# Dilated attention in a hybrid decoder layer: a head's combination in twelve pieces, regroup copies one per two groups, a pool for w_out's raw tiles, and ones-products of one convolution tile moved

## The chip, the cores and the metric

The kernel runs on one core of a Trainium2 chip, as a single program without any communication. The metric is the device time in microseconds (us) of one execution, compared before and after the change. The core has five engines with instruction queues of their own: TensorE (PE, matrix products; its weight loads are listed apart as PEld), VectorE (DVE), ScalarE (ACT), GpSimd (POOL) and SyncE (SP, which in this kernel only issues transfers). An engine works through its own queue in order; between engines there are only semaphores.

## The reference

One decoder layer, 2048 positions of 1024 channels in float32, 8 attention heads of 64:

```python
h = rms_norm(x, g_mix)
u, gb, gc, q, k, v = split(h @ w_in)                  # 3 x 512 conv, 3 x 512 attention
y_conv = gb * short_conv(gc * u, conv_w)              # depthwise, causal, width 3
q = rms_norm(q per head, g_q) * HEAD_DIM ** -0.5
k = rms_norm(k per head, g_k)
for window, dil in ((128, 1), (512, 4), (2048, 16)):  # query t: keys t, t-dil, ..., t-window
    o[b], lse[b] = dilated_branch(q, k, v, window, dil)
y_attn = sum(softmax(lse over b)[b] * o[b])
mix = concat(rms_norm(y_conv, g_conv_out), rms_norm(y_attn, g_attn_out))
x = x + mix @ w_out
h = rms_norm(x, g_ffn)
x = x + (silu(h @ w_gate) * (h @ w_up)) @ w_down
```

## The kernel before

A float32 product is made of three float16 ones: each operand is split into a high and a low half, and high by high, high by low and low by high are summed (`mm3_steps`, lines 191 to 193, and `product` in `project`, L1205). So nearly every operand needs a cast on ACT (the high half) and a subtraction on DVE or POOL (the low half).

**The stages**, by their place in the profiled execution: norms and the first of four convolution tiles (0 to 125 us); the projection to q, k and v (125 to 371); the attention (371 to 722); W_out (to 960); the feed-forward part (to the end; it has no line of the change).

**First convolution tile** (`conv_steps` with j = 0). For each of four stretches c of 512 positions it makes three products (`gemm(2)`, `gemm(0)`, `gemm(1)`), then squares the result on ACT into a tile `c2` (L1356, two buffers). The sum of squares over channels is taken on PE, by four products of one column each with a tile of ones (`squares`, L358, into a PSUM tile `tr` of one buffer). The sums of stretch c-1 are made between `gemm(0)` and `gemm(1)` of stretch c. Those of the last one are made inside the projection's first unit (`last_squares` in `project`). Tiles 1 to 3 run later, in the attention, with j > 0.

**Projection.** Sixteen units, `project(g, c)`: four head pairs g by four stretches of 512 rows. Each has 4 x 48 products into PSUM tiles (`cvx` and `mm`), which ACT scales out into `f` (L1221); then the norms of q and k, in which DVE, ACT and POOL take turns, the split into halves (ACT's L1250 into `qkhl`), and the stores to DRAM, `d_v` (L1232) and `d_qk` (L1254). Beside it weights are prepared, one step per unit by the table `jobs`. `operands` makes the next pair's weights, `spill_conv` writes those of a convolution tile to `d_wc`, `spill_out` splits a part of w_out and writes it to `d_wo`. A step loads its raw data (spill_out: two tiles of 128x4x256, L1287) in one unit; in the next it takes their largest magnitude on DVE (`vmax`, L96), scales and casts them on ACT, subtracts on POOL and stores. Raw tiles and halves of `spill_out`, and the halves of `spill_conv`, all come from one name, `t4`, in the pool `tmp` with three buffers, so a load into it waits until an earlier tile has been stored.

**Attention** (`attn_steps`). Per pair of heads: two heads h, each with the branches b = 1 (dilation 4), 2 (dilation 16) and 0 (dilation 1), in 8, 4 and 8 groups: 40 groups a pair, 160 in all, a count that goes through. A group is: scores on PE (L1467), exponential on ACT (L1472), the mask on POOL (one or two `affine_select`, L1480), the high half on ACT (L1483), the low half on DVE (the subtraction L1484, tile `et`). The product with v (L1494) is issued three groups later (`late`). After every four query tiles DVE copies the result out of PSUM into a tile `u` (L1499, L1502). PE's remaining time in a group is filled by convolution tiles 1 to 3 and the first part of W_out, as a second generator that is advanced at a fixed rate.

The branches 1 and 2 work on permuted positions. Their results go to DRAM and come back in order as tiles `r` (`bring`, L1519). When a head's last branch is done, `combine` adds the three (L1417, L1418, on POOL), takes the smallest denominator into `dmin` (L1420), the reciprocal and a factor (L1421 to L1423, on DVE), multiplies (L1427, POOL), and stores to `d_y` (L1430, SP). It does so in two halves of eight position tiles, each in two steps. The four steps stand in `todo` and fall due at groups n+4 to n+7, where n is the head's last group: a step's instructions are pinned behind that group's mask by `issue_after(sel.ins)`.

Branches 1 and 2 also need q in permuted order: `regroup` makes it from `qT` by four DVE copies (L1380) into a `q16` tile of two buffers. It is called at a pair's group 9, for its second head, and at group 33, for the next pair's first head, without any pin.

**What sets the order.** The program is written in one order, and a scheduler with a timing model of its own then orders each engine's queue: an instruction may be moved ahead of others as soon as its data and buffers allow it, except where `issue_after` holds it. So the regroup copies stand, in the compiled order, where their buffer comes free: in the branch b = 2 of a head, where the combination of the head before also stands.

Of the kernel before, what the change touches and what calls it, by code (L numbers as in the profile page):

```python
# [30 lines left out]
class Builder:  # L31
# [170 lines left out]
    def run(self):  # L202
        tc, nc, A = self.tc, self.nc, self.A
        with ExitStack() as ctx:
# [16 lines left out]
            self.dmin = cp.tile([P, 18], F32, name="dmin")  # L221
# [789 lines left out]
class Fast(Builder):  # L1011
# [22 lines left out]
    def in_and_conv(self):  # L1034
# [5 lines left out]
        with ExitStack() as c:  # L1040
# [42 lines left out]
            n = -1  # L1083
            for step in self.conv_steps(0, W, before):
# [3 lines left out]
                if n == 6:  # L1088
                    norms.close()
                    with tc.issue_after(self.act.ins):  # L1090
                        nc.scalar.preload_act_table_set("natural_log_exp_and_others")
                    self.ring = e(tc.tile_pool(name="ring", bufs=8, side="right"))
# [13 lines left out]
            for n in range(16):  # L1106
# [3 lines left out]
                with ExitStack() as behind:  # L1110
# [13 lines left out]
                    if n == 14:  # L1124
                        self.regroup(self.st0, 0)
# [57 lines left out]
    def project(self, g, c, W):  # L1183
# [27 lines left out]
        def last_squares():  # L1211
            if (g, c) == (0, 0):
                self.squares(3, self.last, self.pstr.tile([P, 4], F32, name="tr"), False)
# [66 lines left out]
    def spill_out(self, half, m):  # L1280
# [4 lines left out]
        for q in range(2):  # L1285
            raw = self.tmp.tile([P, 4, 256], F32, name="t4")
# [22 lines left out]
    def conv_steps(self, j, W, before=None):  # L1309
# [4 lines left out]
        for c in range(4):  # L1314
# [19 lines left out]
            if late is not None:  # L1334
                self.squares(c - 1, late, self.few() if j else self.pstr.tile([P, 4], F32, name="tr"), j > 0)
# [19 lines left out]
            s2 = self.sq[c] if j == 1 else self.cs.tile([P, 512], F32, name="c2", bufs=2)  # L1355
# [5 lines left out]
            late = s2 if j in (0, 3) else None  # L1361
        self.last = late
# [12 lines left out]
    def regroup(self, st, h):  # L1375
# [3 lines left out]
        for n in range(4):  # L1379
            self.nc.vector.tensor_copy(t[:, :, 32 * n:32 * n + 32],  # L1380
                                       st["qT"][:, h, 512 * n:512 * (n + 1)].rearrange("p (a r) -> p r a", r=NT))

# [15 lines left out]
    def attn_steps(self, g, st, nx):  # L1398
# [7 lines left out]
        for h, b in [(h, b) for h in range(2) for b in (1, 2, 0)]:  # L1406
# [4 lines left out]
            def combine(c, n, h=h, last=last):  # L1411

                ts = slice(c, c + n)
                bm = self.at.tile([P, NT], F32, name="bm", bufs=2)[:, 0:n]
                X = [r[:, ts] for r in (U[h, 0], R[h, 1], R[h, 2])]
                e = nc.vector if last else nc.gpsimd
                e.tensor_tensor(X[1], X[1], X[2], op=ALU.add)  # L1417
                e.tensor_tensor(X[0], X[0], X[1], op=ALU.add)  # L1418
                d = 2 * (2 * g + h) + c // n
                nc.vector.tensor_reduce(self.dmin[:, d:d + 1], X[0][:, :, HD], axis=AX.X, op=ALU.min)  # L1420
                nc.vector.tensor_scalar_max(bm, X[0][:, :, HD], 2.0 ** -7)  # L1421
                nc.vector.reciprocal(bm, bm)
                nc.vector.tensor_scalar_mul(bm, bm, uv)  # L1423
                if not last:
                    yield
# [469 lines left out]
```

## Time and profile before

| | |
|---|---|
| median of 3 runs | 2126.46 us (2121.56 to 2128.05) |
| profiled execution: time, span | 2120.59 us, 2118.8 us |
| PE busy | 2019.1 us, 95% |
| DVE busy | 1348.2 us, 64% |
| ACT busy | 1008.9 us, 48% |
| POOL busy | 775.3 us, 37% |
| moved by DMA | 317.02 MB |
| granted TensorE clock, mean | 0.99 |

The profile is one execution on the chip. A group's row reads: line, engine, operation, written tile <- read tiles, shape and type, xcount | busy us, mean ns of one | idle time of that engine just before these instructions, and what ended most of it. A timeline's row reads: start and length in us, engine, line, operation, tiles, xcount, and in brackets the wait ahead of it. Times are from the start of the span. "SPq" is an issue of SP's queue. The bracket `[4.20 <-DVE et L1484]` means that the engine stood idle for 4.20 us and that the tile `et`, written by DVE at L1484, ended it.

The page's share of busy time of PE in 40 equal slices (53 us each), in tenths:

```profile
PE   4999989999899899989999999999999999999998
```

The attention lies in slices 8 to 14.

### The profile page before, as it was taken

Reading aid. Unit: us, or ns where it says so; the run is one execution under the profiler, and the core shown is the slowest. Engines: PE = TensorE matmul, PEld = TensorE weight load, DVE = VectorE, ACT = ScalarE, POOL = GpSimd, SP = SyncE. Lnnn points to the kernel's source line nnn. Section 1 sums busy time; section 2 is a strip of 40 time slices with the busy share of each in tenths; the row PEclk is TensorE's granted clock in tenths of the full one; section 3 lists DMA queues with packets and bytes.
Section 4 is the critical chain, followed back from the end, with each engine's and each line's share of the span. In section 5 each row is a group of like instructions: output and inputs, shape, how many; then the busy total and the mean of one; then the engine's idle time right before and its main releaser. Section 6 shows DMA issues by size and latency. Waiting matters only on the chain.

```text
span 2118.8 us, 34786 instructions
## 1 busy us (share of the span) xinstructions
PE 2019.1 (95%) x13368; PEld 1123.8 (53%) x13368; DVE 1348.2 (64%) x2515; ACT 1008.9 (48%) x1780; POOL 775.3 (37%) x809
## 2 busy tenths in 40 slices
PE   4999989999899899989999999999999999999998
PEld 2499989666566544434444444444444444444443
DVE  7455443567777866886767676676768575555453
ACT  7446655666566566552434333334333344343341
POOL 0026535457666521222212212231222245555463
PEclk9999999999999999999999999999999999999999
DMA  9558984356857567995333223322322762431442
GB/s 242 151 136 213 247 205 121 106 151 133 180 139 218 152 191 230 260 296 160 110 109 105 82 92 105 115 87 93 110 100 90 273 238 60 142 117 55 149 140 81
DMA packets 460272, 317.02 MB, mean 150 GB/s; under 512 B 255681, under 2 KB 413377, under 8 KB 457921
## 3 DMA queue, kind: packets, MB, share of 16 engines
q1 hardware_dynamic: 442416, 291.56, 48.4%
q10 hardware_dynamic: 17680, 23.16, 3.0%
q8 instruction: 106, 1.74, 0.3%
q14 instruction: 70, 0.57, 0.1%
HBM read 157.96 MB, written 116.85 MB: 130 GB/s over the span
## 4 chain that ended last, share of the span: by engine, by line
PE 65%; DVE 10%; DMA 8%; ACT 6%; issue 4%; POOL 4%; SPq 3%; DVEq 0%; ACTq 0%; POOLq 0%
PE ps L812 34%; PE ps L945 15%; PE mm L191 3%; PE mm L192 3%; PE mm L193 3%; POOL sm L1480 2%; PE cvx L1205 2%; PE s L1467 1%; PE av L1494 1%; SPq L199 1%; PE mm L1205 1%; DVE vm_a L96 1%; DMA nx_x<-in_x_dram 1%; DVE et L1484 1%; DMA b<-d_h 1%
## 5 line engine op out<-in xcount | busy, mean ns | idle before, releaser
L812 PEld LDWEIGHTS <-w 128*128 128x128 f16 x3696 | 362.2, 98 | 450.7 <-issue 15.3
L812 PE MATMUL ps<-b,w 128*128 128x512 f16 x2112 | 465.4, 381 | 9.9 <-ACT s L863 5.4
L945 PE MATMUL ps<-b,w 128*128 128x512 f16 x1848 | 399.7, 379 | 2.4 <-DVE x L953 1.2
L812 PE MATMUL ps<-hb,w 128*128 128x512 f16 x1584 | 347.1, 379 | 0.8 <-ACT s L863 0.8
L945 PEld LDWEIGHTS <-w 128*128 128x128 f16 x1848 | 180.8, 98 | 221.1 <-issue 3.5
L1205 PEld LDWEIGHTS <-b 128*128 128x128 f16 x3072 | 255.0, 98 | 9.8 <-issue 9.3
L705 POOL TENSOR_TENSOR t<-wq 128x512 f32<-128x512 f32 (+1 forms) x46 | 59.7, 1297 | 407.2 <-issue 230.6
L1480 POOL TENSOR_SCALAR_AFFINE_SELECT sm<-sm 128x256 f32<-128x256 f32 (+2 forms) x288 | 142.2, 517 | 119.9 <-ACT sm L1472 105.8
L818 DVE TENSOR_TENSOR s<-ps,s 128x512 f32<-128x512 f32 x220 | 150.1, 683 | 38.3 <-PE ps L812 37.8
L1484 DVE TENSOR_TENSOR et<-sm,et 128x512 f16<-128x512 f32 (+1 forms) x160 | 129.3, 816 | 67.1 <-ACT et L1483 65.4
L952 POOL TENSOR_TENSOR x<-x,s 128x512 f32<-128x512 f32 x72 | 103.1, 1432 | 171.3 <-DVE s L966 132.2
L1205 PE MATMUL cvx<-w,b 128*128 128x192 f16 x1776 | 151.2, 246 | 0.7 <-ACT f L1221 0.6
L1483 ACT CAST et<-sm 128x512 f16<-128x512 f32 (+1 forms) x160 | 93.8, 589 | 93.3 <-POOL sm L1480 92.3
L953 DVE SCALAR_TENSOR_TENSOR x<-ps,a_u,x 128x512 f32<-128x512 f32 x96 | 71.8, 749 | 101.1 <-PE ps L945 74.3
L1472 ACT ACTIVATE sm<-s,bound,kap 128x512 f32<-128x512 f32 (+1 forms) x160 | 118.6, 747 | 25.9 <-PE s L1467 21.7
L192 PE MATMUL mm<-b,wq 128*128 128x512 f16 x320 | 122.7, 384 | 0.0
L193 PE MATMUL mm<-b,wq 128*128 128x512 f16 x320 | 122.7, 383 | 0.0
L191 PE MATMUL mm<-b,wq 128*128 128x512 f16 x320 | 122.6, 383 | 0.0
L1205 PE MATMUL mm<-w,b 128*128 128x192 f16 x1296 | 113.1, 248 | 8.2 <-ACT f L1221 8.2
L722 ACT CAST w<-t 128x512 f16<-128x512 f32 x88 | 53.7, 616 | 128.6 <-PE ps L812 86.6
L1494 PE MATMUL av<-v,et 128*128 128x65 f16 x1800 | 86.2, 195 | 27.6 <-DVE et L1484 20.4
L96 DVE TENSOR_REDUCE vm_a<-wq 128x1 f32<-128x2048 f32 (+2 forms) x32 | 77.4, 2417 | 41.0 <-DMA wq<-in_w_up_dram 19.8
(289 smaller groups left out, 3242.1 us busy)
## 6 DMA issues: line engine op xcount, KB each, us to landing
d_a<-a ACTq DMA_DIRECT2D x88, 256.0 KB, 2.0
d_wd<-w SPq DMA_DIRECT2D x77, 256.0 KB, 2.0
wq<-d_a SPq DMA_DIRECT2D x64, 256.0 KB, 4.1
b<-d_wd SPq DMA_DIRECT2D x14, 1024.0 KB, 6.6
wq<-in_w_in_dram SPq DMA_DIRECT2D x24, 512.0 KB, 6.5
d_qk<-qkhl SPq DMA_DIRECT2D x16, 768.0 KB, 4.8
d_h<-hl SPq DMA_DIRECT2D x24, 512.0 KB, 3.1
wq<-in_w_gate_dram SPq DMA_DIRECT2D x22, 512.0 KB, 4.7
```

What stands on the lines that cost most here:

```text
L191: self.pe = mm(ps, lhsT=lh(k), rhs=rh(k), start=k == ks[0], stop=False)
L192: mm(ps, lhsT=lh(k), rhs=rl(k), start=False, stop=False)
L193: mm(ps, lhsT=ll(k), rhs=rh(k), start=False, stop=k == ks[-1])
L812: nc.tensor.matmul(ps[self.BANK[n]], lhsT=w[:, x, k], rhs=b[:, y, k], start=first and k == 0 and q == 0, stop=k == 3 and q == 2, skip_grou ...
L818: nc.vector.tensor_tensor(t, x, y, op=ALU.add)
L945: nc.tensor.matmul(ps[self.BANK[n]], lhsT=L[n][:, x, f], rhs=B[n][:, f, y], start=first and f == 0 and q == 0, stop=f == n_f - 1 and q == ...
L952: nc.gpsimd.tensor_tensor(o, o, s_, op=ALU.add)
L1205: self.pe = nc.tensor.matmul(ps[:, 192 * t:192 * (t + 1)], lhsT=lh(x, k), rhs=w[:, y, k], start=start and t + k + q == 0, stop=stop and k ...
L1472: nc.scalar.activation(e, sp[:, 0:o], AF.Exp, scale=self.kap, bias=self.bound)
L1480: sel = nc.gpsimd.affine_select(m, m, pattern=pattern, compare_op=ALU.is_ge, fill=0.0, base=0, channel_multiplier=-sg)
L1484: nc.vector.tensor_tensor(et[:, 1], e, et[:, 0], op=ALU.subtract)
L1494: self.pe_av = nc.tensor.matmul(ps[:, us.index(u)], lhsT=p_, rhs=v_, start=n_ == 0, stop=n_ == len(ops) - 1)
```

## The change

It has four parts, which touch each other little.

**Combination.** `combine` takes chunks of four position tiles instead of eight and yields after every POOL operation. For each of the four chunks: the first addition is a step; the second addition with the four small DVE operations is a step. Then come four steps of a product and its store. These twelve steps fall due one per group, at n+2 to n+13 instead of n+4 to n+7. `dmin` grows to 32 columns, and `u` gets a fourth buffer. The last head (on DVE, at the end of the attention) keeps its operations.

**Regroup.** `regroup` becomes a generator that yields after each copy. Its copies are issued one at a time at groups 9, 11, 13, 15 and 32, 34, 36, 38 of a pair, each pinned behind that group's subtraction (`issue_after(low.ins)`).

**Raw tiles.** `spill_out` takes its raw tiles from a new pool `raws` with two buffers, and no longer from `t4`.

**Ones-products.** For the first convolution tile the sums of squares of stretches 0 to 2 are not taken between the products any more. Their `c2` tiles (now four buffers) are kept in a list, and `last_squares` makes all four sums in the projection's first unit. Tiles 1 to 3 are as before.

```diff
-            self.dmin = cp.tile([P, 18], F32, name="dmin")
+            self.dmin = cp.tile([P, 32], F32, name="dmin")
...
-            n = -1
+            n, self.sums = -1, []
...
+                    self.raws = e(tc.tile_pool(name="raws", bufs=2, side="right"))
...
-                        self.regroup(self.st0, 0)
+                        for _ in self.regroup(self.st0, 0):
+                            pass
...
         def last_squares():
             if (g, c) == (0, 0):
-                self.squares(3, self.last, self.pstr.tile([P, 4], F32, name="tr"), False)
+                for k in range(4):
+                    self.squares(k, self.sums[k], self.pstr.tile([P, 4], F32, name="tr"), False)
...
-            raw = self.tmp.tile([P, 4, 256], F32, name="t4")
+            raw = self.raws.tile([P, 4, 256], F32, name="raw")
...
-            if late is not None:
-                self.squares(c - 1, late, self.few() if j else self.pstr.tile([P, 4], F32, name="tr"), j > 0)
+            if late is not None and j:
+                self.squares(c - 1, late, self.few(), True)
...
-            s2 = self.sq[c] if j == 1 else self.cs.tile([P, 512], F32, name="c2", bufs=2)
+            s2 = self.sq[c] if j == 1 else self.cs.tile([P, 512], F32, name="c2", bufs=2 if j else 4)
...
+            if j == 0:
+                self.sums.append(s2)
...
             self.nc.vector.tensor_copy(t[:, :, 32 * n:32 * n + 32],
                                        st["qT"][:, h, 512 * n:512 * (n + 1)].rearrange("p (a r) -> p r a", r=NT))
+            yield
...
-            def combine(c, n, h=h, last=last):
...
+            def combine(chunks, e, h=h, last=last):
+
+                bm = self.at.tile([P, NT], F32, name="bm", bufs=2)
+                X = U[h, 0], R[h, 1], R[h, 2]
+                for c in chunks:
+                    ts = slice(c, c + 4)
+                    e.tensor_tensor(X[1][:, ts], X[1][:, ts], X[2][:, ts], op=ALU.add)
+                    yield
+                    e.tensor_tensor(X[0][:, ts], X[0][:, ts], X[1][:, ts], op=ALU.add)
+                    d, w = 4 * (2 * g + h) + c // 4, X[0][:, ts, HD]
+                    nc.vector.tensor_reduce(self.dmin[:, d:d + 1], w, axis=AX.X, op=ALU.min)
+                    nc.vector.tensor_scalar_max(bm[:, ts], w, 2.0 ** -7)
+                    nc.vector.reciprocal(bm[:, ts], bm[:, ts])
+                    nc.vector.tensor_scalar_mul(bm[:, ts], bm[:, ts], uv)
+                    yield
+                for c in chunks:
+                    ts = slice(c, c + 4)
+                    x = X[0][:, ts, 0:HD]
+                    y = self.y7[:, ts] if last else x
+                    e.tensor_tensor(y, x, bm[:, ts].unsqueeze(2).broadcast_to([P, 4, HD]), op=ALU.mult)
+                    if not last:
+                        i = (2 * g + h) * HD
+                        nc.sync.dma_start(self.d_y.rearrange("(t p) c -> p t c", p=P)[:, ts, i:i + HD], y)
+                    yield
+            Ub = U[h, b] = self.up.tile([P, NT, HD + 1], F32, name="u", bufs=4)
...
-                    nc.vector.tensor_tensor(et[:, 1], e, et[:, 0], op=ALU.subtract)
+                    low = nc.vector.tensor_tensor(et[:, 1], e, et[:, 0], op=ALU.subtract)
...
-                            for i, step_ in enumerate(c for m in (0, 8) for c in [combine(m, 8)] * 2):
-                                self.todo.append((self.n + 4 + i, lambda step_=step_: next(step_, None)))
+                            steps = combine((0, 4, 8, 12), nc.gpsimd)
+                            for i in range(12):
+                                self.todo.append((self.n + 2 + i, lambda: next(steps)))
...
                     if count == 9:
-                        self.regroup(st, 1)
-                    if count == 33 and g < 3:
-                        self.regroup(nx, 0)
+                        order = self.regroup(st, 1)
+                    if count == 32 and g < 3:
+                        order = self.regroup(nx, 0)
+                    if count in (9, 11, 13, 15, 32, 34, 36, 38):
+                        with self.tc.issue_after(low.ins):
+                            next(order, None)
```

The changed kernel's lines stand 3 to 14 further down: in its rows L1423, L1425 and L1436 are the additions and the product of the combination, L1490 the mask, L1494 the subtraction, L1385 the regroup copy, L1512 the copy out of PSUM.

How this moves instructions on POOL, at the combination of a second head pair's first head. Before:

```order
L1417 TENSOR_TENSOR r_7017<-r_7017,r_7158 128x520
L1418 TENSOR_TENSOR u<-u,r_7017 128x520
L1480 AFFINE_SELECT sm<-sm 128x2x128 x2
L1480 AFFINE_SELECT sm<-sm 128x512
L1417 TENSOR_TENSOR r_7017<-r_7017,r_7158 128x520
L1427 TENSOR_TENSOR u<-u,bm 128x8x64
L1418 TENSOR_TENSOR u<-u,r_7017 128x520
L1480 AFFINE_SELECT sm<-sm 128x512 x2
```

Changed, the same head:

```order
L1423 TENSOR_TENSOR r_7043<-r_7043,r_7192 128x260
L1490 AFFINE_SELECT sm<-sm 128x2x128 x2
L1425 TENSOR_TENSOR u<-u,r_7043 128x260
L1490 AFFINE_SELECT sm<-sm 128x2x128 x2
L1423 TENSOR_TENSOR r_7043<-r_7043,r_7192 128x260
L1490 AFFINE_SELECT sm<-sm 128x2x128 x2
L1425 TENSOR_TENSOR u<-u,r_7043 128x260
L1490 AFFINE_SELECT sm<-sm 128x512
```

Up to three operations of eight tiles stood between two groups' masks; now one operation of four tiles stands there.

On DVE, at the same place, before:

```order
L1420 TENSOR_REDUCE dmin<-u 128x1
L1421 TENSOR_SCALAR bm<-u 128x8
L1380 COPY q_8304<-qT 128x16x32 x3
L1422 RECIPROCAL bm<-bm 128x8
L1380 COPY q_8304<-qT 128x16x32
L1502 COPY u<-av 128x260
L1423 TENSOR_SCALAR bm<-bm,uv 128x8
L1484 TENSOR_TENSOR et<-sm,et 128x512 x2
```

Changed, where the next regroup's copies stand:

```order
L1494 TENSOR_TENSOR et<-sm,et 128x384
L1385 COPY q_7762<-qT 128x16x32
L1512 COPY u<-av 128x260
L1494 TENSOR_TENSOR et<-sm,et 128x512 x2
L1385 COPY q_7762<-qT 128x16x32
L1512 COPY u<-av 128x260
L1494 TENSOR_TENSOR et<-sm,et 128x512 x2
L1385 COPY q_7762<-qT 128x16x32
L1494 TENSOR_TENSOR et<-sm,et 128x512
```

Four copies stood together amid a combination's small operations; now each has a subtraction on both sides.

On SP, which issues the loads, in the projection at the last w_out step, before:

```order
L1277 DMA d_wc_131<-t_2905 128x2048
L1600 DMA wq<-d_wc_129 128x6144
L1287 DMA t_2911<-in_w_out_dram 128x4x256
L199 DMA_TRANSPOSE ka<-d_qk_133 128x2x512
L199 DMA_TRANSPOSE kb<-d_qk_133 128x2x512
L1254 DMA d_qk_133<-qkhl 128x4x768
```

Changed:

```order
L1309 DMA d_wo_82<-t_2627 128x4x256
L1290 DMA raw<-in_w_out_dram 128x4x256
L1235 DMA d_v_62<-vs_962 128x4x130 x2
L1309 DMA d_wo_82<-t_2633 128x4x256
L1290 DMA raw<-in_w_out_dram 128x4x256
L1257 DMA d_qk_133<-qkhl 128x4x768
```

The second raw load (L1287) stood behind a convolution tile's weight store (L1277) and a large load (L1600); now both raw loads (L1290) are issued with the stores of the w_out step before (L1309), over ten issues earlier.

More of the change, by code (lines that the diff above doesn't have):

```diff
@@ L1409, in attn_steps @@
             last = g == 3 and h == 1
-            def combine(c, n, h=h, last=last):
[L1413 to L1424, printed above, removed]
-                    yield
-                y = self.y7[:, ts] if last else X[0][:, :, 0:HD]
-                e.tensor_tensor(y, X[0][:, :, 0:HD], bm.unsqueeze(2).broadcast_to([P, n, HD]), op=ALU.mult)
-                if not last:
-                    i = (2 * g + h) * HD
-                    nc.sync.dma_start(self.d_y.rearrange("(t p) c -> p t c", p=P)[:, ts, i:i + HD], y)
@@ L1431, in attn_steps @@
-            Ub = U[h, b] = self.up.tile([P, NT, HD + 1], F32, name="u", bufs=3)
+            def combine(chunks, e, h=h, last=last):
[4 more added lines that the diff above has]
+                    e.tensor_tensor(X[1][:, ts], X[1][:, ts], X[2][:, ts], op=ALU.add)
+                    yield
+                    e.tensor_tensor(X[0][:, ts], X[0][:, ts], X[1][:, ts], op=ALU.add)
[14 more added lines that the diff above has]
+                    yield
@@ L1503, in output @@
                         if last and b == 0:
-                            for _ in combine(us[0], 4):
+                            for _ in combine(us[0:1], nc.vector):
                                 pass
```

## The prediction

> **What bounds the kernel now.** I read the busy time by stage first, then what TensorE (PE) waited for, then the engines' timelines around the longest waits. By stage (columns: length, then busy time and instructions of PE, weight load, VectorE (DVE), ScalarE (ACT), GpSimd (POOL), granted clock, DMA):
>
> ```profile
> 125.00:371.00 246.00, 237.21 (x2848) 236.28 (x2846) 118.00 (x263) 145.47 (x272) 121.61 (x105) 0.99 0.72 184
> 371.00:722.00 351.00, 323.59 (x3583) 213.98 (x3582) 249.69 (x456) 224.04 (x377) 217.08 (x344) 0.98 0.60 151
> ```
>
> PE is the bound in both stages that the change touches: 237 of 246 us in the projection, 324 of 351 in the attention. So the change can only win idle PE time, 9 and 27 us. What PE waited for, the first three lines in 370 to 745 us, the last in 0 to 370 us (us in total, times, the longest):
>
> ```profile
> PE av L1494 <- DVE et L1484: 20.4, 17, 4.2
> PE av L1494 <- DVE u L1502: 5.1, 3, 2.0
> PE av L1494 <- DVE u L1499: 1.2, 1, 1.2
> PE mm L1205 <- ACT f L1221: 8.2, 1, 8.2
> ```
>
> The attention's idle time is 26.7 us in 21 waits, all for DVE. The longest, in the timelines of POOL, DVE and PE:
>
> ```profile
> 525.40 1.49 POOL L1427 TENSOR_TENSOR u<-u,bm 128x512 f32<-128x512 f32 x1
> 526.85 1.74 POOL L1418 TENSOR_TENSOR u<-u,r 128x520 f32<-128x520 f32 x1
> 528.54 1.69 POOL L1480 TENSOR_SCALAR_AFFINE_SELECT sm<-sm 128x512 f32<-128x512 f32 x2
> 529.12 3.21 DVE L1380 COPY q<-qT 128x512 f16<-128x512 f16 x3
> 532.36 0.94 DVE L1380 COPY q<-qT 128x512 f16<-128x512 f16 x1
> 533.69 2.13 DVE L1484 TENSOR_TENSOR et<-sm,et 128x512 f16<-128x512 f32 x2
> 534.43 0.73 PE L1494 MATMUL av<-v,et 128*128 128x65 f16 x10 [4.20 <-DVE et L1484]
> ```
>
> A group's mask (L1480) stands behind POOL's combination of the last head, 3.2 us in a row here, and the subtraction that completes the weights (L1484) behind four regroup copies, 4.2 us. PE's product comes three groups after the scores, some 6 us, and this is more delay than that covers.
>
> **After a long wait PE is slow too.** Two rows of PE behind the projection's wait, the busy time around the attention's three longest, and two rows of the last of these:
>
> ```profile
> 292.57 5.88 PE L1205 MATMUL mm<-w,b 128*128 128x192 f16 x48 [8.16 <-ACT f L1221]
> 298.29 4.12 PE L1205 MATMUL cvx<-w,b 128*128 128x192 f16 x48
> 530.00:540.00 10.00, 5.80 (x42) 3.32 (x43) 7.87 (x12) 3.10 (x5) 5.78 (x8) 0.66 0.74 191
> 576.00:584.00 8.00, 4.37 (x38) 2.52 (x37) 6.80 (x13) 2.36 (x5) 3.83 (x4) 0.79 0.76 184
> 705.00:714.00 9.00, 5.48 (x46) 3.09 (x45) 8.64 (x26) 4.21 (x7) 4.22 (x5) 0.81 0.95 207
> 708.08 0.91 DVE L51 SCALAR_TENSOR_TENSOR cvr_t<-cvr_y 128x8 f32<-128x8 f32 x1
> 709.65 0.73 PE L1494 MATMUL av<-v,et 128*128 128x65 f16 x10 [2.33 <-DVE et L1484]
> ```
>
> The same 48 matmuls take 5.88 us after the wait and 4.12 later: a restart costs 1.76 us. The attention has three stretches with a granted clock under 1, so 3 x 1.76 = 5.3 us hang on its stalls beside the 26.7. The last has another reason too: there DVE also works off the small operations that end the convolution (L51), and these stay.
>
> The Trainium skill (TensorE: Matmul & The Clock Gate, "The HAM clock gate") says that the array falls to half rate after an idle window of about 3.4 us and comes back after as long a busy one. The 4.20 and the 8.16 us stalls agree; in 705 to 714 us the clock fell though no single wait there is that long. By the rule alone only the two long stalls would cost, and the gain would be 1.8 us smaller.
>
> **Combination in twelve pieces.** Removed per head: four POOL additions of 128x520 and two products of 128x512; added: eight of 128x260 and four of 128x256, one per group from the second group on instead of four bursts from the fourth. Costs by operation, in 371 to 722 us but for L1484's row, which is the page's (count | busy, mean ns):
>
> ```profile
> L1417 POOL TENSOR_TENSOR r<-r,r 128x520 f32<-128x520 f32 x14 | 20.8, 1487 | 0.0
> L1427 POOL TENSOR_TENSOR u<-u,bm 128x512 f32<-128x512 f32 x14 | 19.6, 1397 | 10.0 <-DVE bm L1423 7.5 <-DVE cvr_t L52 2.0 <-DVE ssa L362 0.5
> L1480 POOL TENSOR_SCALAR_AFFINE_SELECT sm<-sm 128x256 f32<-128x256 f32 x210 | 96.8, 481 | 112.9 <-ACT sm L1472 100.2 <-DVE et L1484 5.3 <-DVE u L1502 3.8
> L1484 DVE TENSOR_TENSOR et<-sm,et 128x512 f16<-128x512 f32 (+1 forms) x160 | 129.3, 816 | 67.1 <-ACT et L1483 65.4
> L1502 DVE COPY u<-av 128x260 f32<-128x260 f32 x61 | 25.6, 422 | 8.8 <-PE av L1494 8.3
> L1380 DVE COPY q<-qT 128x512 f16<-128x512 f16 x24 | 19.5, 858 | 0.0
> L1423 DVE TENSOR_SCALAR bm<-bm,uv 128x8 f32<-128x8 f32 x14 | 6.7, 479 | 0.2
> L1421 DVE TENSOR_SCALAR bm<-u 128x8 f32<-128x8 f32 x14 | 5.4, 385 | 0.0
> L1422 DVE RECIPROCAL bm<-bm 128x8 f32<-128x8 f32 x14 | 2.7, 194 | 0.1
> L1420 DVE TENSOR_REDUCE dmin<-u 128x1 f32<-128x8 f32 x14 | 2.2, 159 | 4.9 <-POOL u L1418 4.9
> ```
>
> A half-size addition is estimated at 1487/2 = 0.74 us. POOL then has 0.74 + 2 x 0.48 = 1.70 us per group. A group without stalls lasts (351 - 26.7 - 5.3)/160 = 1.99 us, so POOL fits, and no mask stands behind more than one piece. DVE gets 14 more sets of four small operations; a set is 0.48 + 0.39 + 0.19 + 0.16 = 1.22 us, 17 us in all at most: 249.7 + 17 = 267 of then 319 us, 84%, as the cover for them.
>
> **Regroup copies, one per two groups.** Nothing is removed: 24 copies of 0.86 us stay. But no subtraction stands behind more than one. They are also pinned behind a group's subtraction, where before they ran as soon as their buffer was free, in the very groups of the combination. The last of four runs two groups ahead of the head that reads it; its first tiles need only the first two copies, so I cost it at nothing (uncovered: one copy, 0.86 us, seven times, 6.0).
>
> What stays: in the eight groups around a first head's 128x512 branch DVE has per group a subtraction 0.82, 6/8 of an evacuation 0.32, half a copy 0.43, a quarter set 0.30, and 0.28 for the rest (249.7 less 129.3, 96 evacuations of 0.42, 19.5 and 17, over 160 groups): 2.15 us against 1.99. Over eight groups and seven heads that is 9 us if nothing covers it, and nothing if the three groups' lead, 6 us, does. The lead is used up in part by the longer way through POOL, so I take 6, the convolution's end among it. Both ends for the range: 0, and 14 if the operations stretch as in today's bursts (a copy 1.07 for 0.86). **Attention: -(26.7 + 5.3) + 6 = -26 us** (-32 to -18).
>
> **Raw tiles in a pool of their own.** What led to the 8.2 us, in order, from the timelines of SP's queue, DVE and ACT:
>
> ```profile
> 262.12 0.65 SPq L1600 DMA_DIRECT2D wq<-d_wc  x1
> 262.81 1.40 SPq L1287 DMA_DIRECT2D t<-in_w_out_dram  x1
> 264.25 8.09 SPq L199 DMA_TRANSPOSE ka<-d_qk  x1
> 275.50 0.53 SPq L1254 DMA_DIRECT2D d_qk<-qkhl  x1
> 275.52 1.22 DVE L96 TENSOR_REDUCE vm_a<-t 128x1 f32<-128x1024 f32 x1 [3.50 <-DMA t<-in_w_out_dram]
> 282.12 0.71 ACT L1250 CAST qkhl<-row 128x256 f16<-128x256 f32 x2 [12.55 <-DMA d_qk<-qkhl]
> ```
>
> The second raw tile took a buffer that the weights' store had to leave first, was issued behind a large load and landed at 275.5. DVE's queue stood at its maximum until then, and with it the normalisation that POOL and ACT wait for; from 282.1 to PE's restart at 292.6 ACT works off a backlog, and PE's accumulators wait. In the change the raw loads stand in SP's order over ten issues earlier, behind the previous w_out step. DVE then never stands there. The wait goes with its restart: 8.2 + 1.8 = 10.0 us. One condition stays: ACT's L1250 also waits for the store of q and k, issued at 275.50. But ACT's scaling of the raw tiles (L1302) is then done before it, and the evacuation follows it directly; I leave 1.5 us. **Projection: -8.5 us** (-10 to 0).
>
> **Ones-products moved.** Twelve products in three sets leave the gaps of the first convolution tile for the projection:
>
> ```profile
> 78.14 1.05 PE L358 MATMUL tr<-ones,c 128*128 128x1 f32 x8 [1.73 <-ACT c L1356]
> 87.15 0.39 PE L192 MATMUL cvx<-b,wq 128*128 128x512 f16 x1 [2.35 <-DMA b<-kb]
> 113.14 0.98 PE L358 MATMUL tr<-ones,c 128*128 128x1 f32 x8
> 104.29 0.96 DVE L1154 TENSOR_TENSOR w<-wq,w 128x768 f16<-128x768 f32 x1 [4.02 <-ACT w L1153]
> ```
>
> A set takes 0.98 us by its row, less some overlap with its neighbours. Two of them, and the 1.73 us, lay ahead of a wait for the transposed input at 87.15: taking them away only makes that wait longer, to some 2.35 + 1.73 + 2 x 0.9 = 5.9 us. The third lay ahead of the first weights' split at 104.29, which also sets when the projection starts. In the projection PE has no gap but the one above, so three sets come on top: **+2.5 us** (0 if the start moves up, 4.3 if the longer wait costs another restart of 1.8).
>
> **Sum.** 2120.6 - 26 - 8.5 + 2.5 = 2088.6, from the profiled execution (2120.59, its span 2118.8 plus 1.8). The runs' median, 2126.46, is 5.9 above it; if the new runs lie as high it would be 2094.5. I take **2092**, 3.4 above the sum; the rivals' times carry the same 3.4.
>
> **Rivals.** (a) The load, not the bursts, makes DVE late: additions in pieces overlap just as much with DVE. For it: three copies took 3.21 us here, 1.07 each, against 0.86 in the mean. Against: in the wait taken apart above 4.2 us of DVE's delay are the four copies alone. Half the attention's gain, 13 us, goes: 2105. The Trainium skill (GPSIMD Engine Reference, "Key points") says that POOL shares its SBUF interfaces with DVE and contends with DVE instructions of two inputs; it speaks for this case, and the stretched copies agree.
> (b) The projection's stall stays, because the store of q and k lands last: 8.5 us less gain, 2100.
> (c) It doesn't do what it says: the pieces wait for each other and pile up behind the masks again. Attention gains nothing: 2120.6 - 8.5 + 2.5 + 3.4 = 2118, 6.0 us less than before like for like. Against: the order on POOL has one piece between masks.
> (d) Slower: DVE's minimum (L1420) waits in its queue for POOL's second addition, now four times a head. Five of 14 waited 4.9 us in all, 0.98 each; behind a piece and two masks, 0.74 + 0.96 = 1.70, over 28 chunks it is 48 us of DVE time. 267 + 48 = 315 of 319: DVE would be the bound, and up to 48 us would show against the 32 won: 2120.6 + 16 - 8.5 + 2.5 + 3.4 = 2134, 10 more than before. It decides once such a wait exceeds about 1.2 us in every chunk.
>
> **Chances.** Forecast 0.60, (a) 0.17, (b) 0.12, (c) 0.07, (d) 0.04. What a measurement can tell from no change is about 0.3%, 6.4 us: forecast, (a) and (b) win more than that, (c) less, (d) loses more. Faster 0.89, same 0.07, slower 0.04. The range: the parts' bounds give 2120.6 - 32 - 10 = 2079 to 2120.6 - 18 + 4.3 = 2107, and the median's 5.9 us on top 2113; 2080 to 2114 takes in (a) and (b).
>
> **What would show it.** Right: PE's waits for et and u in the attention under 10 us, no clock under 0.9 there; no wait of PE for f at L1221's place over 2 us; the wait for b near 85 us grown to 5 us; the projection's first units longer by 0.9 us a set. Wrong: DVE idle on POOL over 20 us (d), waits for et still over 15 us (a), ACT standing for the q and k store while PE stands (b).

## The result

Before 2127.26 us median of 4 runs (2121.56 to 2129.67), changed 2103.55 us median of 4 (2101.05 to 2104.83): a ratio of 0.9891, 95% interval 0.9869 to 0.9913, some 23 us or 1.1% faster. The time lies inside the stated range, 11.6 us above the 2092 that was forecast. The profiled execution of the changed kernel took 2101.05 us, span 2099.3. The ratios in this document leave out three executions that were far longer than all others (2651.47 us in e2, 3686.33 in e4, 6768.1 of the kernel before), and the one profile of e4 is such an execution.

Busy time by stage in the profile after, projection and attention (columns as in the prediction), and under it the same two stages of before, cut at their own boundaries:

```profile
103.00:363.00 260.00, 257.63 (x3107) 256.86 (x3106) 125.49 (x270) 153.94 (x286) 125.39 (x113) 1.00 0.74 184
363.00:708.00 345.00, 330.57 (x3693) 218.73 (x3692) 252.76 (x547) 229.75 (x388) 234.52 (x391) 1.00 0.63 158
```

```profile
105.00:371.00 266.00, 257.13 (x3084) 256.05 (x3083) 125.14 (x273) 151.96 (x282) 122.31 (x110) 0.99 0.71 183
371.00:735.00 364.00, 334.54 (x3692) 220.72 (x3691) 260.75 (x492) 231.63 (x391) 221.92 (x352) 0.98 0.60 152
```

The projection takes 260 us instead of 266 with the same PE work: its idle time went from 9 to 2 us. The attention takes 345 instead of 364, and PE's granted clock is 1.00 in it. PE's waits after, attention first, then the projection:

```profile
PE av L1504 <- DVE et L1494: 8.6, 19, 1.2
PE av L1504 <- DVE u L1512: 2.5, 2, 1.6
PE av L1504 <- DVE u L1509: 1.5, 1, 1.5
...
PE cvx L1207 <- ACT f L1224: 1.2, 2, 0.7
PE mm L1207 <- ACT f L1224: 0.9, 1, 0.9
```

The long stalls are gone (the longest in the attention is 1.6 us, before 4.2), but 12.6 us of short ones are left, where the forecast left 6 and its sign of being right was under 10.

**Where the time went, product by product.** PE's products stand in the same order in both kernels, apart from the twelve ones-products. So the time from one product to another can be compared between profiles. The table does so in us, with three profiles of before and two of after (two of the first and one of the second are the runs c1, c2 and c3 below). The columns are PE's products by number, without the ones-products: the first convolution tile and two thirds of the projection (0 to 2400), the rest of the projection (to 3385), the attention in three parts (to 5000, 6000, 7070), W_out (to 8000), the start of the feed-forward part (to 9000), the rest.

```
              0    2400    3385    5000    6000    7070    8000    9000
           to 2400  3385    5000    6000    7070    8000    9000   13303
before      253.5   92.3   156.6   103.0   110.9   220.6   218.1   931.8
before c1   253.8   90.5   156.6   102.9   108.4   224.1   218.9   931.2
before c2   254.4   91.8   157.5   103.5   108.3   224.9   219.7   933.7
after       254.3   84.3   151.4    91.4   107.8   224.4   221.6   932.9
after c3    254.5   84.9   151.3    91.3   108.5   223.5   222.2   934.6
difference   +0.5   -6.9    -5.5   -11.8    -1.1    +0.8    +3.0    +1.5
```

The difference of the means is 19.5 us in all. The projection gave 6.9, the attention 18.4, nearly all of it in its first two parts; 5.3 us were lost behind the attention, most of it at the start of the feed-forward part.

The groups that the change touches, after, then three rows for comparison: the subtraction of 128x512 before, and the regroup copy in e1 (the combination in pieces alone) and in e2 (the regroup alone), two of the runs below. All are of the attention alone, with the shapes kept apart:

```profile
L1423 POOL TENSOR_TENSOR r<-r,r 128x260 f32<-128x260 f32 x28 | 25.1, 895 | 0.0
L1425 POOL TENSOR_TENSOR u<-u,r 128x260 f32<-128x260 f32 x28 | 24.6, 878 | 0.0
L1494 DVE TENSOR_TENSOR et<-sm,et 128x512 f16<-128x512 f32 x120 | 93.9, 785 | 49.4 <-ACT et L1493 48.9
L1494 DVE TENSOR_TENSOR et<-sm,et 128x384 f16<-128x384 f32 x40 | 24.1, 602 | 19.2 <-ACT et L1493 18.9
L1385 DVE COPY q<-qT 128x512 f16<-128x512 f16 x28 | 20.8, 743 | 0.0
...
L1484 DVE TENSOR_TENSOR et<-sm,et 128x512 f16<-128x512 f32 x120 | 107.1, 900 | 48.5 <-ACT et L1483 47.3
...
L1380 DVE COPY q<-qT 128x512 f16<-128x512 f16 x24 | 20.4, 904 | 0.0
...
L1381 DVE COPY q<-qT 128x512 f16<-128x512 f16 x28 | 19.8, 707 | 0.0
```

A half-size addition costs 0.89 us, not half of 1.49. In exchange DVE's work is quicker: the subtraction of 128x512 takes 785 ns instead of 900, the regroup copy 743 instead of 858. The smaller subtraction, 128x384, is slower, 602 ns instead of 563. The two gains don't have one source. The subtraction of 128x512 is quicker with the pieces alone (794 ns in e1, 905 in e2), the copy with the regroup alone (707 ns in e2, 904 in e1).

### The profile page after: what moved, and what is told of

Read it like the earlier page. It is cut to its first block, busy times and chain, and to the rows that moved or that the text cites. A ratio compares the mean times of both kernels' runs of the same rounds, so it can differ in the third digit from the quotient of the medians.

```text
span 2099.3 us, 34898 instructions
## 1 busy us (share of the span) xinstructions
PE 2014.3 (96%) x13368; PEld 1119.9 (53%) x13368; DVE 1344.3 (64%) x2571; ACT 1008.7 (48%) x1780; POOL 793.5 (38%) x851
## 5 line engine op out<-in xcount | busy, mean ns | idle before, releaser
L1490 POOL TENSOR_SCALAR_AFFINE_SELECT sm<-sm 128x256 f32<-128x256 f32 (+2 forms) x288 | 150.0, 543 | 99.9 <-ACT sm L1482 90.4
L818 DVE TENSOR_TENSOR s<-ps,s 128x512 f32<-128x512 f32 x220 | 150.2, 683 | 35.8 <-PE ps L812 35.3
L1494 DVE TENSOR_TENSOR et<-sm,et 128x512 f16<-128x512 f32 (+1 forms) x160 | 117.9, 739 | 68.6 <-ACT et L1493 67.8
L193 PE MATMUL mm<-b,wq 128*128 128x512 f16 x320 | 121.3, 379 | 0.0
L192 PE MATMUL mm<-b,wq 128*128 128x512 f16 x320 | 121.2, 379 | 0.0
L191 PE MATMUL mm<-b,wq 128*128 128x512 f16 x320 | 121.2, 379 | 0.0
L96 DVE TENSOR_REDUCE vm_a<-wq 128x1 f32<-128x2048 f32 (+2 forms) x32 | 77.3, 2416 | 53.8 <-DMA wq<-in_w_up_dram 27.1
L1504 PE MATMUL av<-v,et 128*128 128x65 f16 x1800 | 86.1, 194 | 14.4 <-DVE et L1494 8.6
```

Of the source, the lines that this page charges most:

```text
L191: self.pe = mm(ps, lhsT=lh(k), rhs=rh(k), start=k == ks[0], stop=False)
L192: mm(ps, lhsT=lh(k), rhs=rl(k), start=False, stop=False)
L193: mm(ps, lhsT=ll(k), rhs=rh(k), start=False, stop=k == ks[-1])
L818: nc.vector.tensor_tensor(t, x, y, op=ALU.add)
L1490: sel = nc.gpsimd.affine_select(m, m, pattern=pattern, compare_op=ALU.is_ge, fill=0.0, base=0, channel_multiplier=-sg)
L1494: low = nc.vector.tensor_tensor(et[:, 1], e, et[:, 0], op=ALU.subtract)
```

## The experiments

Ratios are to the kernel before on the same chip, with 95% intervals.

**Each part alone (e1 to e4).** Each kernel is the one before with one of the four parts of the diff shown above, and nothing else.

> Only the combination in twelve pieces (with the fourth u buffer and the wider dmin). In the traces the whole change moved PE's instructions by 16.7 us in the attention. Theory A (POOL's bursts ahead of the masks are what made the weights late): at least 11 of these 16.7 us come with this part alone, so about 2116 us against 2127; PE's waits for et and u in the attention fall from 26.7 to under 17 us, and the waits of POOL's masks for the queue ahead of them fall. Theory B (the four copies in a row made them late): under 6 us of gain, 2121 or more, and the stall of some 4 us behind the copies stays.

Measured: 0.9966 (0.9953 to 0.9978), 7 us less. In the profile PE's attention takes 357.5 us, against 369.3 in the mean of the three of before (367.9 to 370.5): 11.8 less.

```profile
PE av L1498 <- DVE u L1506: 10.3, 7, 2.6
PE av L1498 <- DVE et L1488: 5.7, 11, 0.9
```

The waits for the weights `et` nearly vanish, and waits for the copy out of PSUM (`u`, L1506) take their place: the four regroup copies still stand in a row on DVE, now ahead of that copy.

> Only the regroup copies one at a time, each pinned behind a group's subtraction; the combination stays in four steps of eight tiles. Theory A: under 6 us of gain, 2121 us or more, since POOL's bursts stay. Theory B: 11 us or more, about 2116. If e1 and e2 together give clearly less than the 16.7 us of both at once, each hides behind the other: a wait for two late engines ends with the later one.

Measured: 0.995 (0.9937 to 0.9963), 10.6 us less; PE's attention 361.7 us, 7.6 less.

```profile
PE av L1496 <- DVE et L1486: 19.2, 21, 2.8
PE av L1496 <- DVE u L1501: 0.8, 1, 0.8
```

Here the waits for `u` are gone and those for `et` stay at 19 us, shorter each. Both theories hold for their half. The two gains in the attention, 11.8 and 7.6, sum to 19.4, and both parts together have 18.4. So in PE's attention the parts add up, within the 2.6 us by which the three profiles of before differ, and nothing shows one hidden behind the other. Theory A's share for e1 (11 or more) is met in PE's attention but not in the time (7 us, 5 to 10), and its bound for e2 (under 6) is met in neither. By the times e2 gains more than e1, by PE's attention less: which of the two parts is worth more stays open.

> Only the pool of their own for w_out's raw tiles. The forecast's step: PE's wait of 8.2 us for f and its slow restart go, PE's instructions at the projection's end stand 8 us earlier, and the time is 8 us less, about 2119. Rival: the later stages give part of it back, because the loads of the feed-forward weights do not move with PE; then the attention starts 8 us earlier, but the end only 4 to 6 us, about 2122.

Measured: 0.9955 (0.9942 to 0.9967), 9.6 us less. The rest of the projection takes 83.4 us against 91.5 in the mean: 8.1 less, the forecast's step. The rival isn't seen: W_out and the start of the feed-forward part take 224.6 and 219.2, as in c1 and c2.

> Only the ones-products of the first convolution tile moved. The forecast's step: the wait for the transposed input ahead of 87 us grows by what the two sets and their wait took, and three sets come on top in the projection's first unit, 0.85 us each: up to 2.5 us slower, 2127 to 2130. Rival (the start moves up): PE's first projection product starts 2 us earlier, and the balance is 0 to 0.5 us, not to be told from no change.

Measured: 1.0005 (0.9996 to 1.0013), no change; in us from -0.8 to +2.8, so the forecast's 2.5 lies at the upper end.

**The change without the ones-products' move.**

> The change without its fourth part: the ones-products stay between the first convolution tile's products. If they cost what the forecast says (up to 2.5 us), this kernel is 2 us faster than the changed one, near 2101 against 2103.5, a ratio to before of 0.988 against 0.989. If they cost nothing, as the single run of this part suggests (ratio 1.0005), it is the same, 0.989.

Measured: 0.9901 (0.9884 to 0.9918), beside 0.9891 for the whole change: the same. In its profile the first column is 254.2 us, against 254.3 and 254.5 with the move. The move costs nothing that can be told from noise (the two ratios have intervals of some 4 us to each side; the first column is the sharper sign).

**What is left in the attention: the order on ACT, or the load on DVE.** In the changed kernel's timeline, ACT around 442 to 451 us, at the end of the first pair:

```profile
442.26 1.44 ACT L1482 ACTIVATE sm<-s,bound,kap 128x512 f32<-128x512 f32 x2
443.91 0.62 ACT L1493 CAST et<-sm 128x512 f16<-128x512 f32 x1 [0.21 <-POOL sm L1490]
445.67 0.62 ACT L1493 CAST et<-sm 128x512 f16<-128x512 f32 x1 [1.14 <-POOL sm L1490]
446.19 1.44 ACT L1482 ACTIVATE sm<-s,bound,kap 128x512 f32<-128x512 f32 x2
448.22 0.62 ACT L1493 CAST et<-sm 128x512 f16<-128x512 f32 x1 [0.59 <-POOL sm L1490]
449.98 0.62 ACT L1493 CAST et<-sm 128x512 f16<-128x512 f32 x1 [1.14 <-POOL sm L1490]
450.51 0.77 ACT L1482 ACTIVATE sm<-s,bound,kap 128x512 f32<-128x512 f32 x1
```

Two exponentials, two casts, and the next two exponentials stand behind the casts, which wait for POOL's masks, which wait for the exponentials. That is a loop: two groups take 446.19 - 442.26 = 3.93 us, then 4.32. PE issues a group in about 2.1 us, so ACT has no room to catch up, and each piece of the combination between two masks lengthens the loop. The next experiment opens it, on the changed kernel:

```diff
-                    nc.scalar.activation(e, sp[:, 0:o], AF.Exp, scale=self.kap, bias=self.bound)
+                    ex = nc.scalar.activation(e, sp[:, 0:o], AF.Exp, scale=self.kap, bias=self.bound)
+                    if self.pend:
+                        with self.tc.issue_after(ex.ins):
+                            self.pend()                    # cast and subtraction of the group before
...
-                    nc.scalar.copy(et[:, 0], e)
-                    low = nc.vector.tensor_tensor(et[:, 1], e, et[:, 0], op=ALU.subtract)
+                    def pend(et=et, e=e):
+                        nc.scalar.copy(et[:, 0], e)
+                        self.lowi = nc.vector.tensor_tensor(et[:, 1], e, et[:, 0], op=ALU.subtract)
+                    self.pend = pend
```

> The changed kernel, but ACT's cast of a group (and with it DVE's subtraction) pinned behind the next group's exponential; the work is the same. Theory of the loop: in the changed kernel ACT mostly has a group's cast ahead of the next exponential, the cast waits for POOL's mask, and so exponential, mask and cast of one group (0.77 + 0.85 + 0.62 us) must end before the next group's begin, which is longer than a group of 2.05 us; the exponentials' wait behind their scores, 224 us summed over 160 groups, falls under 130, PE's waits for et in the attention fall from 9 to under 4 us, and the time is 4 to 7 us less than the changed kernel's, ratio to before 0.986 or less. Theory of the load (POOL's pieces slow DVE by their mere running): POOL and DVE do the same work beside each other as before, so PE's waits stay within 3 us of what they were and the ratio stays at 0.989.

Measured: 0.9865 (0.9849 to 0.9881), 2094.96 us (2093.43 to 2096.86): faster than both kernels. On the same chip the two other variants of the changed kernel, e5 and e7, had 2102.11 and 2101.05, each with its lowest run above e6's highest. ACT's waits in the changed kernel, with POOL's for ACT between them, then ACT's in this one:

```profile
ACT et L1493 <- POOL sm L1490: 98.3, 116, 2.4
...
POOL sm L1490 <- ACT sm L1482: 90.4, 95, 5.2
...
ACT sm L1482 <- PE s L1477: 4.4, 4, 2.6
```

```profile
ACT sm L1482 <- PE s L1477: 64.5, 86, 2.6
...
ACT et L1497 <- POOL sm L1493: 26.3, 34, 3.3
```

ACT stands for masks 26 us instead of 98; now it mostly stands for scores, that is, it is ahead. In the same stretch as above, one exponential per group, each straight behind its scores:

```profile
444.46 0.78 ACT L1482 ACTIVATE sm<-s,bound,kap 128x512 f32<-128x512 f32 x1 [0.74 <-PE s L1477]
445.13 0.61 ACT L1497 CAST et<-sm 128x512 f16<-128x512 f32 x1
446.47 0.78 ACT L1482 ACTIVATE sm<-s,bound,kap 128x512 f32<-128x512 f32 x1 [0.73 <-PE s L1477]
```

Summed over the 160 groups, the exponentials begin 46 us behind the end of their scores, instead of 224. PE's attention takes 346.1 us, 4.7 less than the mean of the changed kernel's two profiles, with 86.9 instead of 91.4 in the second part. The end of the expectation fell: PE's waits for `et` are still 9.5 us (expected under 4), and they now lie mostly in the last part, which takes 109.7 us against 107.8 and 108.5. PE's listed gaps in the attention fall by only 1.7 us (14.4 to 12.7); most of the other 3 us is time between one product with v and the next, and between the scores and those products, which the view doesn't list as waits. The edit moves DVE's subtraction together with the cast, so it prices the order as a whole. So the loop is shown as a cost, but not as the whole of what is left.

> The changed kernel, but the four small DVE operations once per head for all 16 tiles, behind the last addition, instead of four times: 21 sets fewer in seven heads, some 1.2 us each, 25 us of DVE time. Theory of the load on DVE: PE's waits in the attention fall by 5 us or more, ratio 0.987 or less. Theory of the loop through ACT and POOL: DVE has room, nothing changes by more than 2 us, ratio 0.988 to 0.990. Third, the slower side: the larger operations come in one lump and stand before a subtraction, 2 us or more slower.

```diff
-                    d, w = 4 * (2 * g + h) + c // 4, X[0][:, ts, HD]
+                    if c != chunks[-1]:
+                        yield
+                        continue
+                    ts = slice(chunks[0], c + 4)
+                    d, w = 2 * g + h + (c // 4 if last else 0), X[0][:, ts, HD]
```

Measured: 0.9896 (0.988 to 0.9912), as the changed kernel's 0.9891; PE's attention 351.5 us against 350.6 and 351.0. Taking 21 sets of small operations off DVE, by which its busy time in the attention fell from 258 to 244 us, brings nothing: DVE's load by itself isn't what is left.

> The kernel before, with nothing of the change, but with ACT's cast pinned behind the next group's exponential. If the loop through ACT and POOL is something that the pieces of the combination brought (the exponentials' wait rose from 112 to 224 us with the change), this gains at most 2 us on the kernel before, ratio 0.999 or more. If the loop held the attention before too, beside the bursts, it gains 4 to 7 us as it did on the changed kernel, ratio 0.997 or less.

The edit is that of e6, on the kernel before. Measured: 0.9974 (0.9963 to 0.9985), 5.5 us less. ACT's waits in a profile of before (c1), then here:

```profile
ACT et L1483 <- POOL sm L1480: 92.3, 99, 2.9
ACT sm L1472 <- PE s L1467: 21.5, 23, 2.4
```

```profile
ACT sm L1472 <- PE s L1467: 68.3, 87, 5.1
ACT et L1487 <- POOL sm L1483: 28.3, 35, 2.3
```

The first of the two expectations falls (0.999 lies outside the interval), the second stands, with 0.997 inside it: the loop was there before the change too, and opening it pays about the same. The change doubled the exponentials' lag, from 112 to 224 us, but did not bring the loop.

**A longer lead.** The changed kernel with the products four groups behind the scores:

```diff
-                    et = self.ep.tile([P, 2, 512], F16, name="et", bufs=5)[:, :, 0:o]
+                    et = self.ep.tile([P, 2, 512], F16, name="et", bufs=6)[:, :, 0:o]
...
-                    if len(late) > 3:
+                    if len(late) > 4:
```

> The changed kernel, but PE's products come four groups after the scores instead of three (and et has six buffers); all orders between exponential, mask, cast and subtraction stay free as in the changed kernel. In the changed kernel 37 of 160 groups need over 6 us from the scores' end to the weights, which is what three groups cover. If the remaining 14 us of waits are late single groups (latency), 8 us of lead cover nearly all of them: PE's waits for et and u in the attention fall under 6 us, its time is 6 to 10 us less than the changed kernel's, ratio 0.987 or less. If the loop through ACT and POOL is slower than PE over many groups (throughput), a longer lead only moves the waits back: gain under 3 us, ratio 0.988 to 0.990, and the summed time from scores to weights grows.

Measured: 0.9893 (0.9877 to 0.991), no gain on the changed kernel.

```profile
PE av L1504 <- DVE u L1512: 9.6, 9, 2.4
PE av L1504 <- DVE u L1509: 4.0, 3, 1.5
...
PE av L1504 <- DVE et L1494: 0.3, 1, 0.3
```

The waits for `et` are gone, and waits for the copy out of PSUM take their place, 13.6 us. The summed time from scores to weights grows from 838 to 954 us, as a loop that is too slow over many groups would have it. But the new wait is another one, so this run alone doesn't separate the two readings. Ahead of the two longest, 2.36 and 2.12 us, the copy stands in DVE's queue behind a regroup copy of 1.67 us and the combination's small operations, and behind the small operations that end the convolution. PE's clock also fell behind these two (0.86 in 600 to 612 and in 700 to 712 us), some 3.4 us that the changed kernel doesn't lose.

**Is time given back behind the attention?** From the first two profiles it looked so: W_out took 220.6 us before and 224.4 after. Three more profiles tell:

> The kernel before once more, for a second profiled execution. Since the first one, at 2120.59 us, lies 3 us under the median of its runs, two readings of the stages behind the attention differ: if the loads of the feed-forward weights give time back when PE comes earlier, the stretch from the attention's end to the ninth thousand of PE's instructions takes again the 439 us of the first profile, against 446 in the changed kernel; if the first profile was a quick execution there, it takes 442 to 446 us here.

> The kernel before a third time, for the same question: 439 us from the attention's end to the ninth thousand of PE's instructions if the changed kernel gives time back there, 442 to 446 if the first profile was a quick one.

> The changed kernel once more, for a second profiled execution: the stretch from the attention's end to the ninth thousand of PE's instructions takes 444 to 448 us again if that is its own length, 440 to 443 if it varies from one execution to the next.

Measured, W_out and the start of the feed-forward part together: 443.0 and 444.6 us for the kernel before, 445.7 for the changed one, where the first profiles had 438.7 and 446.0. So the first profile of before was a quick one in W_out, and nothing is given back there. At the start of the feed-forward part, 218.1 to 219.7 before against 221.6 and 222.2 after, 3.0 us are lost. PE stands there for DVE's work on finished accumulators (L818). In the profile after, one such wait of 2.05 us lies behind a maximum over weights (L96) that had itself waited 1.25 us for its load. That looks like a give-back, but e9, whose PE arrives just as early, takes 217.8 us. What sets these 3 us stays open.

## Why the prediction was right, and where it was off

The direction and the range held. The range was wide enough to hold the rivals (a) and (b) too, so the time alone doesn't choose between them. By its own steps:

- **What bounds the kernel** held: PE's idle time and its slow stretches behind long waits were won, in the projection and in the attention, and nothing else.
- **Restarts of the clock** held. The attention's time less PE's listed gaps fell by 4.8 us (341.0 to 336.2 in the two first profiles); the sum had 5.3 for three restarts. The granted clock is 1.00 in the attention. (The 4.8 us also hold whatever PE lost between products without a listed gap; no run separates the two.)
- **Raw tiles** held, -6.9 us in the difference of the means and -8.1 alone, where the sum had -8.5. The order is as read from the rows: the two raw loads are issued at 238.63 and 241.98 instead of up to 262.81, DVE's maximum runs without a wait, and 2.1 us of PE's waits for `f` are left (1.5 in the sum). This is the third of four w_out steps, not the last, as it is called ahead of the prediction. In all four together DVE's maximum had waited 20.9 us for raw loads before; now it waits in none.

```profile
238.63 1.12 SPq L1290 DMA_DIRECT2D raw<-in_w_out_dram  x1
241.98 0.67 SPq L1290 DMA_DIRECT2D raw<-in_w_out_dram  x1
...
259.34 2.33 DVE L96 TENSOR_REDUCE vm_a<-raw 128x1 f32<-128x1024 f32 x2
```

- **Ones-products**: +2.5 us in the sum, +0.5 in the first column and nothing in e4 and e5. The 0.84 us that each set adds to the projection's first unit is there: 0.98 by its row, with the next product at 114.56. What failed is the term ahead of it: the start moved up. From PE's first product to the projection's first it took 79.8 to 80.4 us in the three profiles of before and takes 78.7 and 79.2 now. I expected the wait for `b` to take all of what was removed and grow to 5.9; it is still 2.30, and another of 1.64 us lies ahead of it.

```profile
83.25 0.38 PE L191 MATMUL cvx<-b,wq 128*128 128x512 f16 x1 [1.64 <-ACT cu L1345]
85.93 0.39 PE L192 MATMUL cvx<-b,wq 128*128 128x512 f16 x1 [2.30 <-DMA b<-kb]
...
113.72 0.98 PE L358 MATMUL tr<-ones,c 128*128 128x1 f32 x8
```

- **The residual of the attention** is the term that was mis-sized: 6 us in the sum (up to 14), and 14.4 us of PE's gaps in the profile after, 2.3, 5.1 and 7.0 in its three parts. The attention won 18.4 us instead of 26, just inside its bounds of 18 to 32. That it stayed inside is in part luck: the loop below was not in the working at all. I worked the residual out from DVE's busy time per group against PE's, and took the three groups' lead as cover. Two things were missing. First, busy time isn't what limits a group: exponential, mask and cast form a loop through two in-order queues. It costs some 5 us (e6, e8), and e7 shows that DVE's load doesn't. POOL's side of it was priced too low: a piece at 0.74 us and two masks at 0.48 made 1.70 us per group, where the trace has 0.89 and, for the 216 masks of 128x256 (L1490), 0.53, so 1.95. Second, the last part won 1.1 us only: it had 6.2 us of gaps ahead of the products with v before and has 7.0 now. There DVE works off the end of the convolution and the combination's small operations between the copies out of PSUM. That is read from the rows; no run takes the convolution's end out, and e7, with fewer of the combination's small operations, takes no less there (109.5 us). The prediction named the convolution's end for one stall and had 6 us for all three parts together:

```profile
681.61 1.12 DVE L1350 SCALAR_TENSOR_TENSOR cg<-cu,convw,cg 128x512 f32<-128x512 f32 x1
682.65 0.69 DVE L53 SCALAR_TENSOR_TENSOR cvr_y<-cvr_t,cvr_y 128x8 f32<-128x8 f32 x1
683.26 0.15 DVE L1427 TENSOR_REDUCE dmin<-u 128x1 f32<-128x4 f32 x1
...
683.40 0.41 DVE L1509 COPY u<-av 128x260 f32<-128x260 f32 x1
...
683.86 0.53 PE L1504 MATMUL av<-v,et 128*128 128x65 f16 x12 [1.51 <-DVE u L1509]
```

  One reading under this term was also off, without much effect. The group length of 1.99 us was taken from 371 to 722 us, but the last product with v starts at 734.4. Up to 735 us the same working gives 2.07 us for PE and 2.21 for DVE, and about 8 us uncovered instead of 9.

- **The sum** was 2088.6, made against one profiled execution; the profile after took 2101.05. By the means above the 12.4 us between are the attention (7.6), the projection (1.6) and the stages behind the attention, which the sum left alone (5.3), less the 2.0 that the ones-products didn't cost.

The rivals: (a), half the attention's gain for the load's sake, gave 2105 and so came nearest to the measured time, but not for its reason. DVE's busy time in the attention fell (260.8 to 252.8 us) although the pieces brought it more operations, and taking load off DVE did nothing (e7). The stretched copies that it was argued from go with where the copies stand: with the pieces alone, still in a row, they took 904 ns. (b) fell with e3, where 8.1 of the 8.5 us came, (c) with the attention's waits, 12.6 us instead of 26.7. (d) fell with DVE's waits for the second addition, 3.7 us in all where it needed more than 1.2 us in every chunk:

```profile
DVE dmin L1427 <- POOL u L1425: 3.7, 5, 1.3
```

The restart of the clock can be read once more in the profile after, behind the attention, from PE's timeline and the busy time around it:

```profile
714.63 0.38 PE L193 MATMUL mm<-b,b 128*128 128x512 f16 x1
717.52 0.39 PE L191 MATMUL ps<-b,b 128*128 128x512 f16 x1 [2.50 <-ACT b L585]
...
718.51 0.63 PE L192 MATMUL ps<-b,b 128*128 128x512 f16 x1
...
714.00:722.00 8.00, 5.50 (x18) 2.00 (x17) 5.45 (x15) 5.98 (x15) 1.27 (x1) 0.79 0.14 48
```

One wait of 2.50 us, after products without a gap (PE is busy 6.00 of the 6.00 us from 708 on), and the next ones take 0.63 us instead of 0.38 at a granted clock of 0.79. That is some 1.7 us lost in these 8 us, about the restart of 1.76 that the prediction read before the change. The Trainium skill (TensorE: Matmul & The Clock Gate, "The HAM clock gate") has the array fall to half rate after some 3.4 us without work; by that this wait would cost nothing beside itself. The measurement decides: this shorter wait cost a restart too.

## What to carry to other kernels

A chain that goes through two in-order engines and comes back to the first is a loop if the first engine's queue holds the chain's end ahead of the next round's start. Its length is the sum of the durations on both engines, and it limits the rate even where each engine has room; the view of waits shows it as one engine waiting for the second nearly as long as the second waits for the first (98 and 90 us here; 26 and 71 in e6, with the loop opened). The kernel before had the same sign, 92 us in c1 for ACT on POOL, before anything was changed. Put the next round's start ahead of this round's end before counting busy time.

Before a stage is said to give time back, take a second and a third profile of the kernel before: a stage that the change doesn't touch differed by 4 us between executions.

## What the runs showed of the hardware

Two things weren't expected. Additions on POOL cut in half take 895 and 878 ns, 60% and 57% of the whole ones' 1487 and 1543, so pieces cost POOL some 14 to 20% more in sum; how much of it is a fixed cost per instruction and how much is work beside DVE, no run here separates. And the time of the same operation on DVE depends on where it stands. The subtraction of 128x512 went from 900 to 785 ns, and to 794 with POOL's pieces alone; the one of 128x384 went the other way, from 563 to 602. The regroup copy went from 858 to 743 ns, to 707 when only its place changed, and to 904 when only POOL's operations were cut. That POOL's operations beside it make the difference is argued, not shown.
